# Trunk kernel: a third row pair of gate and up in seven products, T loaded first, and some pairs without accumulating DMA

## The chip, the cores and the metric

The kernel runs on one core of a Trainium2 chip. The core has a matrix engine (PE in the profile), a vector engine (DVE), a scalar engine (ACT), a general engine (POOL, GpSimd) and a sync engine (SP, which here only issues DMAs). Each of them works off its own list of instructions in order and waits on semaphores for the others. The metric is the device time of one execution in microseconds (us); lower is better.

## What is computed

The reference is a trunk of two residual layers on 256 tokens of width 2048, with float32 inputs and weights. Each layer is a token mixer (HGRN2 in layer 0, gated linear attention, GLA, in layer 1) together with a cross-attention into 256 memory tokens, an output projection, and a SwiGLU feed-forward part. Cut to what matters here:

```python
for layer in range(2):
    hn = _rmsnorm(h, norm_mix[layer])
    y, xq = _hgrn2_mixer(...) if layer == 0 else _gla_mixer(...)
    xa = _memory_attention(xq, mem_n, w_mem_kv[layer])
    h = h + concatenate([y, xa]) @ w_out[layer]
    hn = _rmsnorm(h, norm_ffn[layer])
    gate, up = split(hn @ w_gate_up[layer], 2)      # w_gate_up: 2048 x 11264
    h = h + (silu(gate) * up) @ w_down[layer]       # w_down: 5632 x 2048
return _rmsnorm(h, norm_final)
```

Nearly all of the work is products of the 256 tokens with weights that are read once from device memory.

## The kernel before

**Precision.** A float32 weight tile is split into a high and a low part (`split`, L276): ACT copies it rounded into the high part, and DVE (or, once a block, POOL, through `free_port`) subtracts to get the low part. A product of an activation factor (also in two parts) with a weight tile is then three matmuls of 128x128 by 128x512. Split tiles lie in a ring of six buffers (`parts`) or, if single, of two (`part`).

**Seven products instead of eight.** Two wanted results (for instance gate and up, or two column groups of one matrix) for two token tiles from two row tiles of weights form a 2x2 by 2x2 block product: eight products the plain way, seven by a Strassen-Winograd scheme. The kernel takes the 16 row tiles of a weight in eight *pairs* p = 0..7. A pair has one of three kinds:

- **O**: eight products. `raw` holds four weight tiles of 128x512, which are split in two halves a and b (two ACT casts and two DVE subtractions of 128x1024).
- **S**: seven products (`seven`, L427). DVE also forms sums of weight tiles: it needs T, the sum of the two c1 tiles, then T minus the c0 tile (a 128x512 subtraction on `raw`), two more differences (128x1024 on `raw`), and six split tiles instead of four (named a, b, c and d). T itself is made by DMA: after the plain loads, POOL issues a DMA that adds the second c1 tile onto `raw[:, 1]` (`accum_op=add`, L425).
- **H**: eight products that are spread over the same seven accumulators as S; DVE has one more subtraction and one more split tile than for O.

**The feed-forward part** (`ffn`, L1178) works in 11 blocks of 512 columns a layer. For each block `project_halves` (L597) runs through the eight pairs; a string of `KINDS` (L1167) gives their kinds: one string each for blocks 0 to 3, the last one for blocks 4 to 10. `PAIRS` (L360) says which sums of activation tiles are prepared for each pair: those of S (eight factors), of O (six, among them d1, which only O uses) or of both (B). H uses factors that S has too. After block b come two *downs* of earlier blocks (L1218): w_down times finished columns, accumulated onto h. Seven DVE additions (`sums`, L1187) put a block's seven accumulators together while the downs run. When a down is done, ACT copies its two results from the matrix engine's banks back to h (`give_back`, L1232).

**What sets the order.** From block 1 on (and from pair 3 of block 0) every engine's order is the program's own (`Engine.kept`); elsewhere a scheduler orders the instructions. Loads go through `load_pair` (L413), issued by SP, into a ring of three `raw` tiles of four weight tiles each: pair p+3 is loaded into the tile that pair p leaves when DVE has read it for the last time (its tile d for S). All compute instructions show as L151, a helper's line, so that groups are told apart by tile names: `f_p` are the accumulators of a block, `fd` those of a down, `partsNa` to `partsNd` the split tiles of load number N, `raw` the loaded tiles. In the GLA mixer `gg..p` and `gk..p` are accumulators.

`project_two` (L522) does the same for the mixers, the output projection and the last downs; there two or three pairs of a projection are S and the others plain.

Of the kernel before, what the change touches and what calls it, by code (L numbers as in the profile page):

```python
# [14 lines left out]
ALU = mybir.AluOpType  # L15
AX = mybir.AxisListType

P = 128
# [10 lines left out]
DK = 192  # L29
# [11 lines left out]
def trunk_kernel(ctx: ExitStack, tc: tile.TileContext, x, mem, norm_mix, norm_ffn, norm_mem,  # L41
                 norm_final, hgrn_w_in, hgrn_lb_logits, hgrn_onorm, gla_w_in, gla_w_gk,
                 gla_b_gk, gla_onorm, w_mem_kv, w_out, w_gate_up, w_down, c_ident, c_mask, out):
    nc = tc.nc
# [312 lines left out]

    PAIRS = "SSOSSOSB"  # L360
    HOMES = (("hq", "hq"),) * 4 + (("F", "K"), ("T", "sc"), ("Q", None), ("v", "gate"))
    FACTORS = {"S": ("x10", "x00", "x01", "x11", "s", "d0", "u", "z"), "O": ("x10", "x00", "x01", "x11", "d0", "d1"),
               "B": ("x10", "x00", "x01", "x11", "s", "d0", "u", "z", "d1")}
# [46 lines left out]

    TIMES = {"S": (1,) * 7, "O": (0, 2, 2, 2, 2, 0, 0), "H": (0, 2, 2, 2, 1, 0, 1)}

    def load_pair(raw, w, p, c0, c1, n, kind):  # L413

        if n_w[0] == 1:
            for k, j, c in ((0, 0, c0), (0, 1, c1), (1, 3, c0), (1, 2, c1)):
                nc.sync.dma_start(out=raw[:, j, 0:n], in_=w[(2 * p + k) * P:(2 * p + k + 1) * P, c:c + n])
                if k == 0 and c == c1:
                    load_mem(0, 256, 512)
            return  # L420
        for j, c in ((slice(1, 3), c1), (slice(0, 4, 3), c0)):
            nc.sync.dma_start(out=raw[:, j, 0:n],
                              in_=w[2 * p * P:(2 * p + 2) * P, c:c + n].rearrange("(k p) c -> p k c", p=P))
        if kind == "S":
            nc.gpsimd.dma_start(out=raw[:, 1, 0:n], in_=w[(2 * p + 1) * P:(2 * p + 2) * P, c1:c1 + n], accum_op=ALU.add)  # L425

    def seven(i, raw, between=None):  # L427

        n = raw.shape[2]
        tt = ve.tensor_tensor  # L430
        b00, = split(raw[:, 0:1, :], f"{i}a")
        b11, b10 = split(raw[:, 2:4, :], f"{i}b")
        if between:
            between()

        tt(out=raw[:, 0, :], in0=raw[:, 1, :], in1=raw[:, 0, :], op=ALU.subtract)
        tt(out=raw[:, 2:4, :], in0=raw[:, 2:4, :], in1=raw[:, 0:1, :].broadcast_to([P, 2, n]), op=ALU.subtract)
        t6, t7 = split(raw[:, 0:2, :], f"{i}c", turned=True)
        t5, t4 = split(raw[:, 2:4, :], f"{i}d")
        return {1: ("x00", b00), 2: ("x01", b10), 3: ("z", b11), 4: ("x11", t4), 5: ("s", t5), 6: ("u", t6), 7: ("d0", t7)}  # L440
# [79 lines left out]
            self.x = lambda k, t: quads[p // 2].x(p % 2 * 2 + k, t)  # L520

    def project_two(pairs, plan, w, c0, c1, n, name, give, view=lambda ps: ps, onto=None, prep=None, behind=None,  # L522
                    base=0):

        ps, out = {}, []  # L530
        if any(c.isdigit() for c in plan):
            order, plan = [base + int(c) for c in plan[::2]], plan[1::2]
        else:
            sevens, plains = iter(range(len(PAIRS))), iter(range(plan.count("S"), len(PAIRS)))
            order = [next(sevens if c == "S" else plains) for c in plan]
        left = {b: plan.count("S") * (b < 8) + 2 * plan.count("-") * (b in (2, 3, 4, 8)) for b in range(1, 9)}

        def product(b, left_factor, right):
            first = b not in ps
            if first:  # L540
                ps[b] = bank(f"{name}p{b}")
            left[b] -= 1
            (xh, xl), (hi, lo) = left_factor, right
            acc = ps[b][:, 0:n]
            pe.matmul(acc, xh, hi, start=first, stop=False)
            pe.matmul(acc, xh, lo, start=False, stop=False)
            pe.matmul(acc, xl, hi, start=False, stop=left[b] == 0)

        def add(to, b, other):
            ve.tensor_tensor(out=to, in0=view(ps[b][:, 0:n]), in1=other, op=ALU.add)  # L550

        def early():
            l, r = give()
            out.extend((l(0), l(1), r(0), r(1)))
            s0, s1, e1, e0 = out
            ac.copy(out=s0, in_=view(ps[1][:, 0:n]))
            add(e1, 6, s0)
            add(s1, 7, e1)
            add(e0, 5, s1)
            add(e1, 5, e1)  # L560
            if onto:
                for to, part in zip(onto, out):
                    ve.tensor_tensor(out=to, in0=to, in1=part, op=ALU.add)
                out[:] = onto

        for at, (p, kind) in enumerate(zip(order, plan)):
            i, raw = new_raw()
            if i == 0:
                load_pair(raw, w, p, c0, c1, n, kind)
            if prep:  # L570
                prep(at)
            if i > 0:
                load_pair(raw, w, p, c0, c1, n, kind)
            if kind == "S":
                todo = held(behind, seven, i, raw[:, :, 0:n]) if behind else seven(i, raw[:, :, 0:n])
                last = at == plan.rindex("S")
                for b in (1, 6, 7, 5, 2, 4, 3) if last else (3, 2, 1, 6, 7, 5, 4):
                    product(b, pairs[p].get(todo[b][0]), todo[b][1])
                if last and at == len(plan) - 1:
                    early()  # L580
                elif len(pending) > MANY:
                    step()
                continue
            b00, b01 = split(raw[:, 0:2, 0:n], f"{i}a", 2 if i else 1)
            b11, b10 = split(raw[:, 2:4, 0:n], f"{i}b")
            if at > 0 and at == plan.rindex("S") + 1:
                early()
            for k, (lf, rt) in enumerate(((b00, b01), (b10, b11))):
                step()
                for b, t, right_factor in ((2, 0, lf), (4, 1, lf), (8, 1, rt), (3, 0, rt)):  # L590
                    if b == 8 and len(pending) > MANY:
                        step()
                    product(b, pairs[p].x(k, t), right_factor)
        for to, b in zip(out, (2, 4, 3, 8)):
            add(to, b, to)

    def project_halves(forms, kinds, w, c0, c1, name, key, keep):  # L597


        left = {b: sum(TIMES[kind][b - 1] for kind in kinds) for b in range(1, 8)}  # L600
        ps = {}

        def product(b, left_factor, right):
            first = b not in ps
            if first:
                ps[b] = bank(f"{name}p{b}")
            left[b] -= 1
            (xh, xl), (hi, lo) = left_factor, right
            pe.matmul(ps[b], xh, hi, start=first, stop=False)
            pe.matmul(ps[b], xh, lo, start=False, stop=False)  # L610
            pe.matmul(ps[b], xl, hi, start=False, stop=left[b] == 0)

        for p, kind in enumerate(kinds):
            Engine.kept = keep <= p
            i, raw = new_raw()
            load_pair(raw, w, p, c0, c1, 512, kind)
            x = forms[p].get
            last = p == len(PAIRS) - 1
            if kind == "S":
                todo = seven(i, raw, lambda: mark(key + p))  # L620
                for b in (1, 2, 6, 7, 5, 4, 3) if last else (1, 3, 2, 6, 7, 5, 4):
                    product(b, x(todo[b][0]), todo[b][1])
            else:
                b00, b01 = split(raw[:, 0:2, :], f"{i}a")
                mark(key + p)
                b11, b10 = split(raw[:, 2:4, :], f"{i}b")
                todo = [[(2, "x00", b00), (5, "x10", b01), (4, "x10", b00), (3, "d0", b01)]]
                if kind == "O":
                    todo.append([(2, "x01", b10), (5, "x11", b11), (4, "x11", b10), (3, "d1", b11)])
                else:  # L630
                    ve.tensor_tensor(out=raw[:, 3, :], in0=raw[:, 3, :], in1=raw[:, 2, :], op=ALU.subtract)
                    e1, = split(raw[:, 3:4, :], f"{i}c")
                    todo.append([(2, "x01", b10), (3, "x01", b11), (7, "x11", b11), (4, "x11", e1)])
                todo = [m for ms in zip(*todo) for m in ms] if last else todo[0] + todo[1]
                for b, f, right in todo:
                    product(b, x(f), right)
            step()
        return ps
# [398 lines left out]
    def gla_pair(w, pr, dec, decay, hq, r, yq):  # L1037
# [40 lines left out]
        def give():  # L1078
            for name in "kq":
# [2 lines left out]
            return [lambda t, d=d: d[:, t, :, 0:DK] for d in dst]  # L1082

        project_two(hq["pairs"], ("------S-", "------S-")[pr], w, kw + pr * 2 * DK, pr * 2 * DK, 2 * DK, f"gk{pr}", give,
                    lambda ps: ps.rearrange("p (a c) -> p a c", c=DK))
        for d in dst:
            for t in range(NT):
                ac.activation(out=d[:, t, :, 0:DK], in_=d[:, t, :, 0:DK], func=AF.Copy, scale=r[:, t:t + 1])
# [7 lines left out]
        for a in range(2):  # L1096
            def give():
                for dst, tag in ((gate, "gate"), (v, "v")):
# [1 line left out]
                return [lambda t, d=d[a]: d[:, t, :] for d in (gate, v)]  # L1100

            project_two(hq["pairs"], GLA[pr][a], w, 2 * kw + MIX + (2 * pr + a) * DV, 2 * kw + (2 * pr + a) * DV, DV,
                        f"gg{pr}{a}", give)
            for dst, func in ((gate[a], AF.Silu), (v[a], AF.Copy)):
                for t in range(NT):
                    ac.activation(out=dst[:, t, :], in_=dst[:, t, :], func=func, scale=r[:, t:t + 1])
# [57 lines left out]
    PARTS = ((0,), (1, 2), (3, 4), (5, 6), (7, 8), (9, 10))  # L1164


    KINDS = ("SHOSHOSO", "HHOSSOSO", "SHOSSOSO", "SSOSSOHS", "SSOSSOSS")  # L1167

# [224 lines left out]
```

## Time and profile before

| what | us |
|---|---|
| median of three runs | 2276.28 |
| lowest and highest of them | 2270.11, 2280.8 |
| the profiled execution | 2272.82 |
| its span, from first to last instruction | 2271.0 |
| PE busy in the span | 2247.5 |
| DVE busy | 1974.3 |
| ACT busy | 1429.7 |
| POOL busy | 210.9 |

The profiled execution lies 3.46 us under the median of the runs and 1.82 us above its own span. The page gives each engine's busy time; the chain of waits follows the end of the program back to its start; the table of windows gives busy time by stretch; the timeline lists single instructions with the idle time before them and what ended it. The stages in time are: memory keys and values to about 105 us, the HGRN2 mixer to 422, output projection to 517, feed-forward of layer 0 to 1211, GLA mixer to 1484, output projection to 1574, feed-forward of layer 1 to the end. PE's granted clock is 1.00 or 0.99 in nearly all of these stretches.

### The profile page before, as it was taken

The page shows a single profiled execution, that of the slowest core. Times are in us where ns is not written, and L with a number is a line of the kernel's source. Part 1 is how long each engine was busy: PE and PEld are TensorE (multiplying, and loading weights), DVE is VectorE, ACT ScalarE, POOL GpSimd, SP SyncE. Part 2 cuts the span into 40 slices and gives each one's busy share as a digit, 9 for nine tenths or more (in the row PEclk, how much of TensorE's full clock was granted, in tenths as well). Part 3 has the DMA queues.
Part 4 walks back from the last instruction along what each step waited for, and adds up shares of the span by engine and source line. Part 5 has one row for each costly group of instructions (what it writes and reads, how often), then busy time and mean ns, then how long its engine had stood idle before and what let it go on. Part 6 is the DMA issues. An engine that isn't in the chain of part 4 may idle for free.

```text
span 2271.0 us, 30130 instructions
## 1 busy us (share of the span) xinstructions
PE 2247.5 (99%) x10710; PEld 1904.3 (84%) x10710; DVE 1974.3 (87%) x2449; ACT 1429.7 (63%) x1938; POOL 210.9 (9%) x215
## 2 busy tenths in 40 slices
PE   9999999999999999999999999999999999999998
PEld 7888888888888888888889899888888888888887
DVE  7889999898898889988996786789888898888997
ACT  7656656565666666666675565567566666666664
POOL 1000100000111111111100000000011111111110
PEclk9999999999999999999999999999999999999999
DMA  8656665656777777777765556466677777777774
GB/s 293 215 170 208 203 184 166 194 195 181 223 233 226 223 231 247 224 215 228 235 211 164 149 161 191 139 212 213 195 222 223 235 231 220 232 230 228 232 240 153
DMA packets 254827, 475.56 MB, mean 209 GB/s; under 512 B 15663, under 2 KB 46419, under 8 KB 254419
## 3 DMA queue, kind: packets, MB, share of 16 engines
q1 hardware_dynamic: 231203, 429.64, 56.1%
q0 software_dynamic: 22176, 39.72, 11.1%
q10 hardware_dynamic: 1296, 4.26, 0.5%
q8 instruction: 84, 1.38, 0.2%
q14 instruction: 68, 0.56, 0.1%
HBM read 470.42 MB, written 3.15 MB: 209 GB/s over the span
## 4 chain that ended last, share of the span: by engine, by line
PE 94%; DVE 2%; DMA 2%; issue 1%; ACT 0%; SPq 0%; POOL 0%; POOLq 0%; DVEq 0%; ACTq 0%
PE f_p L151 39%; PE fd L151 19%; PE wo L151 4%; PE m1p L151 2%; PE hv2p L151 2%; PE hv1p L151 2%; PE hv0p L151 2%; PE wo0p L151 2%; PE wo1p L151 2%; PE hf2p L151 2%; PE hf1p L151 2%; PE fd_0p L151 2%; PE m0p L151 2%; PE gg01p L151 1%; PE hf0p L151 1%; DMA raw<-in_gla_w_in_dram 1%
## 5 line engine op out<-in xcount | busy, mean ns | idle before, releaser
L151 DVE TENSOR_TENSOR raw<-raw 128x512 f32<-128x512 f32 (+3 forms) x320 | 299.0, 934 | 62.7 <-DMA raw<-in_w_gate_up_dram 34.0
L151 DVE TENSOR_TENSOR parts<-raw,parts 128x1024 fp32r<-128x1024 f32 (+1 forms) x196 | 224.3, 1179 | 23.4 <-ACT parts L151 23.0
L151 ACT CAST parts<-raw 128x1024 fp32r<-128x1024 f32 (+1 forms) x216 | 212.6, 1017 | 50.4 <-PE fd L151 6.5
L425 POOL DMA_DIRECT2D raw<-in_w_gate_up_dram x114 | 98.9, 867 | 990.2 <-DMA raw<-in_w_gate_up_dram 670.1
L151 ACT COPY h<-fd 128x512 f32<-128x512 f32 x80 | 46.6, 588 | 79.1 <-PE fd L151 75.8
L292 POOL TENSOR_TENSOR parts<-raw,parts 128x1024 fp32r<-128x1024 f32 x20 | 48.8, 2440 | 204.3 <-ACT parts L151 192.0
L151 ACT ACTIVATE s<-s,rf_r 128x512 f32<-128x512 f32 x44 | 31.8, 723 | 41.9 <-DVE s L151 41.7
L151 DVE TENSOR_TENSOR e<-f_p,e 128x512 f32<-128x512 f32 x66 | 45.3, 686 | 2.6 <-DVE s L151 0.5
L151 ACT COPY fd<-h 128x512 f32<-128x512 f32 x82 | 45.3, 585 | 0.0
L151 PE MATMUL fd<-parts,s_2h 128*128 128x512 f32 x128 | 39.8, 392 | 0.0
L151 PE MATMUL fd<-parts,s_0h 128*128 128x512 f32 x128 | 39.8, 392 | 0.0
L151 PE MATMUL fd<-parts,s_4h 128*128 128x512 f32 x128 | 39.8, 392 | 0.0
L151 PE MATMUL fd<-parts,s_8h 128*128 128x512 f32 x128 | 39.8, 392 | 0.0
L151 PE MATMUL fd<-parts,s_6h 128*128 128x512 f32 x128 | 39.8, 392 | 0.0
L151 PE MATMUL fd<-parts,s_3h 128*128 128x512 f32 x128 | 39.4, 389 | 0.0
L151 PE MATMUL fd<-parts,s_7h 128*128 128x512 f32 x128 | 39.4, 389 | 0.0
L151 PE MATMUL fd<-parts,s_5h 128*128 128x512 f32 x128 | 39.4, 389 | 0.0
L151 PE MATMUL fd<-parts,s_1h 128*128 128x512 f32 x128 | 39.4, 389 | 0.0
L151 DVE TENSOR_TENSOR s<-f_p,e 128x512 f32<-128x512 f32 x44 | 30.3, 690 | 10.1 <-PE f_p L151 8.2
L425 POOL DMA_DIRECT2D raw<-in_hgrn_w_in_dram x17 | 14.8, 872 | 216.0 <-DMA raw<-in_hgrn_w_in_dram 125.9
L151 DVE SCALAR_TENSOR_TENSOR s<-e,rf_r,s 128x512 f32<-128x512 f32 x44 | 31.0, 747 | 0.2
L151 PEld LDWEIGHTS fd<-parts,s_7h 128*128 128x128 f32 x128 | 24.0, 188 | 5.0
(5729 smaller groups left out, 7315.4 us busy)
## 6 DMA issues: line engine op xcount, KB each, us to landing
raw<-in_w_gate_up_dram SPq DMA_DIRECT2D x352, 512.0 KB, 4.2
raw<-in_w_down_dram SPq DMA_DIRECT2D x80, 1024.0 KB, 6.7
raw<-in_hgrn_w_in_dram SPq DMA_DIRECT2D x96, 512.0 KB, 4.2
raw<-in_gla_w_in_dram SPq DMA_DIRECT2D x96, 384.0 KB, 3.3
raw<-in_w_gate_up_dram POOLq DMA_DIRECT2D x114, 256.0 KB, 5.4
raw<-in_w_out_dram SPq DMA_DIRECT2D x16, 1024.0 KB, 5.2
raw<-in_w_out_dram SPq DMA_DIRECT2D x32, 512.0 KB, 4.1
raw<-in_w_mem_kv_dram SPq DMA_DIRECT2D x30, 512.0 KB, 5.6
```

Source lines behind the costliest of these rows:

```text
L151: ins = func(*args, **kwargs)
L292: low = (nc.gpsimd if free_port else ve).tensor_tensor(out=both[:, 1, k:j, 0:m], in0=src[:, k:j, :], in1=both[:, 0, k:j, 0:m].bitcast(F32) ...
L425: nc.gpsimd.dma_start(out=raw[:, 1, 0:n], in_=w[(2 * p + 1) * P:(2 * p + 2) * P, c1:c1 + n], accum_op=ALU.add)
```

## The change

There are three edits.

1. `PAIRS` and `KINDS`: pair 2 of gate and up is prepared as S instead of O. In blocks 4 to 10 it runs as S (seven products). In blocks 0 to 3 it becomes H (eight products, as O).
2. `load_pair` has a flag `fed`. An S pair that is fed now loads T's first tile by a DMA of its own ahead of all others, lets POOL add the second tile onto it, and loads c0's two tiles and the remaining c1 tile after that: three SP DMAs instead of two.
3. An S pair that is not fed has two plain DMAs and no accumulating one; DVE forms T with an addition in `seven`. Not fed are the first pair of each feed-forward block (`fed = p > 0`) and all S pairs of the GLA mixer's `project_two` calls.

```diff
-    PAIRS = "SSOSSOSB"
+    PAIRS = "SSSSSOSB"
...
-    def load_pair(raw, w, p, c0, c1, n, kind):
+    def load_pair(raw, w, p, c0, c1, n, kind, fed):
...
-        for j, c in ((slice(1, 3), c1), (slice(0, 4, 3), c0)):
-            nc.sync.dma_start(out=raw[:, j, 0:n],
-                              in_=w[2 * p * P:(2 * p + 2) * P, c:c + n].rearrange("(k p) c -> p k c", p=P))
-        if kind == "S":
-            nc.gpsimd.dma_start(out=raw[:, 1, 0:n], in_=w[(2 * p + 1) * P:(2 * p + 2) * P, c1:c1 + n], accum_op=ALU.add)
-
-    def seven(i, raw, between=None):
+        if kind == "S" and fed:
+            rows = [w[(2 * p + k) * P:(2 * p + k + 1) * P, c1:c1 + n] for k in range(2)]
+            nc.sync.dma_start(out=raw[:, 1, 0:n], in_=rows[0])
+            nc.gpsimd.dma_start(out=raw[:, 1, 0:n], in_=rows[1], accum_op=ALU.add)
+        nc.sync.dma_start(out=raw[:, 0:4:3, 0:n], in_=w[2 * p * P:(2 * p + 2) * P, c0:c0 + n].rearrange("(k p) c -> p k c", p=P))
+        if kind == "S" and fed:
+            nc.sync.dma_start(out=raw[:, 2, 0:n], in_=rows[1])
+        else:
+            nc.sync.dma_start(out=raw[:, 1:3, 0:n], in_=w[2 * p * P:(2 * p + 2) * P, c1:c1 + n].rearrange("(k p) c -> p k c", p=P))
+
+    def seven(i, raw, fed, between=None):
...
+        if not fed:
+            tt(out=raw[:, 1, :], in0=raw[:, 1, :], in1=raw[:, 2, :], op=ALU.add)
         tt(out=raw[:, 0, :], in0=raw[:, 1, :], in1=raw[:, 0, :], op=ALU.subtract)
...
     def project_two(pairs, plan, w, c0, c1, n, name, give, view=lambda ps: ps, onto=None, prep=None, behind=None,
-                    base=0):
+                    base=0, fed=True):
...
-            load_pair(raw, w, p, c0, c1, 512, kind)
+            fed = p > 0
+            load_pair(raw, w, p, c0, c1, 512, kind, fed)
...
         project_two(hq["pairs"], ("------S-", "------S-")[pr], w, kw + pr * 2 * DK, pr * 2 * DK, 2 * DK, f"gk{pr}", give,
-                    lambda ps: ps.rearrange("p (a c) -> p a c", c=DK))
+                    lambda ps: ps.rearrange("p (a c) -> p a c", c=DK), fed=False)
...
             project_two(hq["pairs"], GLA[pr][a], w, 2 * kw + MIX + (2 * pr + a) * DV, 2 * kw + (2 * pr + a) * DV, DV,
-                        f"gg{pr}{a}", give)
+                        f"gg{pr}{a}", give, fed=False)
...
-    KINDS = ("SHOSHOSO", "HHOSSOSO", "SHOSSOSO", "SSOSSOHS", "SSOSSOSS")
+    KINDS = ("SHHSHOSO", "HHHSSOSO", "SHHSSOSO", "SSHSSOHS", "SSSSSOSS")
```

On DVE, in one of the blocks 4 to 10 of layer 0, the rows from pair 1's last two split tiles (load 173) to pair 3's first (load 175) stood so before (`raw_N` is the loaded tile of a pair):

```order
L151 SCALAR_TENSOR_TENSOR parts173c<-raw_7945,parts173c 128x1024
L151 TENSOR_TENSOR parts173d<-raw_7945,parts173d 128x1024
L151 TENSOR_TENSOR parts174a<-raw_7990,parts174a 128x1024
L151 TENSOR_TENSOR parts174b<-raw_7990,parts174b 128x1024
L151 TENSOR_TENSOR parts175a<-raw_8023,parts175a 128x512
```

The same stretch of DVE's list in the changed kernel:

```order
L151 SCALAR_TENSOR_TENSOR parts173c<-raw_8046,parts173c 128x1024
L151 TENSOR_TENSOR parts173d<-raw_8046,parts173d 128x1024
L151 TENSOR_TENSOR parts174a<-raw_8092,parts174a 128x512
L151 TENSOR_TENSOR parts174b<-raw_8092,parts174b 128x1024
L151 TENSOR_TENSOR raw_8092<-raw_8092 128x512
L151 TENSOR_TENSOR raw_8092<-raw_8092 128x1024
L151 SCALAR_TENSOR_TENSOR parts174c<-raw_8092,parts174c 128x1024
L151 TENSOR_TENSOR parts174d<-raw_8092,parts174d 128x1024
L151 TENSOR_TENSOR parts175a<-raw_8132,parts175a 128x512
```

Pair 2 (load 174) has six DVE instructions where it had two, and the pairs 0 to 4 now form five S pairs in a row.

On SP, at the end of the same block, the loads of pairs 5, 6 and 7 and of the first down (two loads) stood so before (x2: two alike in a row):

```order
L422 DMA raw_8101<-in_w_gate_up_dram 128x2x512 x2
L422 DMA raw_8134<-in_w_gate_up_dram 128x2x512 x2
L422 DMA raw_8173<-in_w_gate_up_dram 128x2x512 x2
L303 DMA raw_8214<-in_w_down_dram 128x4x512
L303 DMA raw_8258<-in_w_down_dram 128x4x512
```

And in the changed kernel, from pair 6 to the first load of the down:

```order
L423 DMA raw_8245<-in_w_gate_up_dram 128x512
L425 DMA raw_8245<-in_w_gate_up_dram 128x2x512
L427 DMA raw_8245<-in_w_gate_up_dram 128x512
L423 DMA raw_8285<-in_w_gate_up_dram 128x512
L425 DMA raw_8285<-in_w_gate_up_dram 128x2x512
L427 DMA raw_8285<-in_w_gate_up_dram 128x512
L303 DMA raw_8327<-in_w_down_dram 128x4x512
```

Each fed pair has three loads; POOL's addition to `raw[:, 1]` waits for the first of them, the 128x512 one, as it waited for the first 128x2x512 one before.

On DVE, around the first S pair of the GLA mixer (load 230, 384 columns), the rows stood so before; `y_3l` is a part of the cross-attention's result and `raw` the loaded tile:

```order
L151 TENSOR_TENSOR parts229a<-raw_10347,parts229a 128x2x384
L151 TENSOR_TENSOR parts230a<-raw_10380,parts230a 128x384
L151 TENSOR_TENSOR raw_10380<-raw_10380 128x384
L151 TENSOR_TENSOR y_3l<-ao_10264,y_3h 128x512
L151 TENSOR_TENSOR y_3l<-ao_10271,y_3h 128x512
```

And in the changed kernel:

```order
L151 TENSOR_TENSOR parts230a<-raw_10519,parts230a 128x384
L151 TENSOR_TENSOR raw_10519<-raw_10519 128x384
L151 TENSOR_TENSOR parts229a<-raw_10486,parts229a 128x2x384
L151 TENSOR_TENSOR raw_10519<-raw_10519 128x384
L151 TENSOR_TENSOR y_3l<-ao_10403,y_3h 128x512
```

DVE has one row on `raw` more, the addition that forms T, and the split tile of the load before (229) has moved in between it and the subtraction that uses T.

More of the change, by code (lines that the diff above doesn't have):

```diff
@@ L568, in project_two @@
             if i == 0:
-                load_pair(raw, w, p, c0, c1, n, kind)
+                load_pair(raw, w, p, c0, c1, n, kind, fed)
             if prep:
@@ L572, in project_two @@
             if i > 0:
-                load_pair(raw, w, p, c0, c1, n, kind)
+                load_pair(raw, w, p, c0, c1, n, kind, fed)
             if kind == "S":
-                todo = held(behind, seven, i, raw[:, :, 0:n]) if behind else seven(i, raw[:, :, 0:n])
+                todo = held(behind, seven, i, raw[:, :, 0:n], fed) if behind else seven(i, raw[:, :, 0:n], fed)
                 last = at == plan.rindex("S")
@@ L619, in project_halves @@
             if kind == "S":
-                todo = seven(i, raw, lambda: mark(key + p))
+                todo = seven(i, raw, fed, lambda: mark(key + p))
                 for b in (1, 2, 6, 7, 5, 4, 3) if last else (1, 3, 2, 6, 7, 5, 4):
```

## The prediction

> **What bounds the kernel now.** I read the busy times first, then the windows, then the chain of waits.
>
> ```profile
> PE 2247.5 (99%) x10710; PEld 1904.3 (84%) x10710; DVE 1974.3 (87%) x2449; ACT 1429.7 (63%) x1938; POOL 210.9 (9%) x215
> 516.85:601.80 84.95, 84.95 (x383) 70.29 (x383) 74.76 (x89) 52.06 (x66) 8.36 (x8) 1.00 0.72 219
> 954.63:1016.73 62.10, 62.10 (x280) 51.53 (x279) 54.12 (x57) 39.40 (x49) 6.78 (x8) 1.00 0.72 217
> 1234.20:1484.00 249.80, 238.76 (x1402) 231.74 (x1401) 191.77 (x317) 146.14 (x229) 14.84 (x22) 0.99 0.55 163
> 971.83 5.46 PE fd L151 x24
> 977.29 39.44 PE f_p L151 x174
> 1016.73 16.32 PE fd L151 x72
> ```
>
> A window's columns are its length, then busy time of PE, PEld, DVE, ACT and POOL, PE's clock, DMA share and rate. PE is busy for all of 84.95 us of the first two blocks and all of 62.10 us of a late block, and the chain of a late block is PE alone: 174 matmuls of the block in 39.44 us, 0.2267 us each, then downs. Only the GLA mixer has idle PE time, 249.80 - 238.76 = 11.0 us. So the change can gain by fewer matmuls, and by up to 11.0 us in GLA; it can lose wherever DVE comes late for PE. DVE is busy for 54 of 62 us there and is the engine to be checked.
>
> **Fewer matmuls.** In 7 blocks of each of 2 layers one product, three matmuls, goes: 42 x 0.2267 = **9.5 us less**. A late block takes 39.44 - 0.68 = 38.76 us of PE, a product 0.68, an S pair 4.76 and an O pair 5.44. In blocks 0 to 3 H has as many products as O, and PE gains nothing.
>
> **DVE in a late block.** The timelines of ACT and DVE in the block above:
>
> ```profile
> 976.70 1.27 ACT L151 COPY h<-fd 128x512 f32<-128x512 f32 x2 [2.31 <-PE fd L151]
> 978.96 1.23 DVE L151 SCALAR_TENSOR_TENSOR parts173c<-raw,parts173c 128x1024 fp32r<-128x1024 f32 x1 [0.96 <-ACT parts173c L151]
> 981.23 1.22 DVE L151 TENSOR_TENSOR parts174a<-raw,parts174a 128x1024 fp32r<-128x1024 f32 x1
> 983.50 0.69 DVE L151 TENSOR_TENSOR parts175a<-raw,parts175a 128x512 fp32r<-128x512 f32 x1
> 989.53 0.69 DVE L151 TENSOR_TENSOR parts176a<-raw,parts176a 128x512 fp32r<-128x512 f32 x1
> 994.71 1.22 DVE L151 TENSOR_TENSOR parts176d<-raw,parts176d 128x1024 fp32r<-128x1024 f32 x1
> ...
> 1008.59 1.95 DVE L151 TENSOR_TENSOR raw<-raw 128x512 f32<-128x512 f32 x2 [2.35 <-DMA raw<-in_w_gate_up_dram]
> 1010.55 1.23 DVE L151 SCALAR_TENSOR_TENSOR parts179c<-raw,parts179c 128x1024 fp32r<-128x1024 f32 x1
> 1011.74 1.23 DVE L151 TENSOR_TENSOR parts179d<-raw,parts179d 128x1024 fp32r<-128x1024 f32 x1
> ```
>
> DVE can't run far ahead: ACT's copy of the last down waits for PE, and behind it ACT makes what DVE's tile 173c needs. So in every block DVE starts pair 2 (load 174) 981.23 - 977.29 = 3.94 us after PE has started pair 0. From there an O pair costs it 983.50 - 981.23 = 2.27 us and an S pair 989.53 - 983.50 = 6.03. Pair 2 as S costs 3.76 more. Pairs 2 to 7 are then S S S O S S: 5 x 6.03 + 2.27 = 32.42, and DVE could go on to the next work 36.36 us after PE's start. Its instructions overlap by some 0.09 us, so its last tile d is written at 36.45, and c 1.19 (1011.74 - 1010.55) before, at 35.26. PE starts pair 7 at 38.76 - 4.76 = 34.00 and uses c after two products, at 35.36, and d after four, at 36.72. **The margin is 0.1 us for c and 0.27 for d.** Before, d was ready at 1012.97 - 977.29 = 35.68, with the wait of 2.35 in it, and needed at 34.68 + 2.72 = 37.40: 1.7 us of margin. So the expected 9.5 us are all there if DVE waits for nothing in a block, and each tenth it waits beyond the first is a tenth of PE's, 14 times.
>
> **What DVE still waits for: T.** By the waits and the DMA issues:
>
> ```profile
> DVE raw L151 <- DMA raw<-in_w_gate_up_dram: 34.0, 42, 2.3
> raw<-in_w_gate_up_dram SPq DMA_DIRECT2D x352, 512.0 KB, 4.2
> raw<-in_w_gate_up_dram POOLq DMA_DIRECT2D x114, 256.0 KB, 5.4
> ```
>
> 42 waits of 0.81 us on average, at most 2.3, all in the subtraction that needs T. Pair 7 is the tightest: its tile is free when 176d ends at 995.93, and T is needed an O pair, an S pair and its own a and b (0.69 and 1.22, overlapping) later, 2.27 + 6.03 + 1.7 = 10.0 us; 4.2 + 5.4 at the medians, and some hand-over, fill that. With T's tile loaded alone and first, POOL's addition starts earlier by what 256 KB less take: 1.2 us at the 217 GB/s of the window above if the pair's loads flow one after the other, nothing if they share the engines and end together. I take the middle, 0.6. That leaves 0.2 of the average wait, and I put **0.25 us a block** on PE for it, 14 x 0.25 = 3.5 us back; the ends are 0 and 2.35 - 0.1 = 2.25.
>
> The Trainium skill (GPSIMD Engine Reference, Key points) says that GpSimd shares its SBUF interfaces with VectorE and contends with DVE instructions that have two SBUF inputs. Nearly all of DVE's here have two, and it will be denser; if that held POOL's descriptor writing back, T would come later and the sum would be that of the third rival below. The row that bears on it:
>
> ```profile
> L425 POOL DMA_DIRECT2D raw<-in_w_gate_up_dram x114 | 98.9, 867 | 990.2 <-DMA raw<-in_w_gate_up_dram 670.1 <-DVE raw L151 101.9 <-DVE h L151 32.6
> ```
>
> A mean of 867 ns beside a DVE that is busy 87% of the time shows no such stretching, so the sum goes without it.
>
> **First pairs and H.** DVE's addition for pair 0 (0.69 us, as the single `raw` subtraction below) comes before the point where DVE waits for ACT (0.96 at 978.96), which hides it; without that cover, and with DVE the bound everywhere, it would cost 0.69 us in each of 20 blocks, 13.8 us. H in place of O costs DVE there:
>
> ```profile
> 616.73 0.69 DVE L151 TENSOR_TENSOR raw<-raw 128x512 f32<-128x512 f32 x1
> 618.11 0.69 DVE L151 TENSOR_TENSOR parts103c<-raw,parts103c 128x512 fp32r<-128x512 f32 x1 [0.69 <-ACT parts103c L151]
> 650.39 0.69 DVE L151 TENSOR_TENSOR s<-f_p,e 128x512 f32<-128x512 f32 x1 [1.79 <-PE f_p L151]
> ```
>
> That is 0.69 + 0.69 of waiting + 0.69 = 2.07 us in 8 blocks. In such a block DVE itself waits 1.79 us for PE before the sums, so I cost it at nothing; the 0.3 that stick out would be 2.2 us in all, the whole without cover 16.6. Pair 2's larger activation form is two small instructions more, twice, beside a PE that is never idle there: nothing. The loads' new order in HGRN2, memory and output projection changes no DVE work, and PE has no wait there that it could remove: nothing, with -1 to +2 for the scheduler's order.
>
> **GLA.** Ten accumulating DMAs go, ten DVE additions of 128x384 come:
>
> ```profile
> L151 DVE TENSOR_TENSOR raw<-raw 128x384 f32<-128x384 f32 x10 | 5.6, 557 | 14.2 <-DMA raw<-in_gla_w_in_dram 10.1 <-issue 3.2 <-DVE parts237a L151 0.5
> PE slg L151 <- DVE GQ L151: 3.5, 2, 2.3
> PE slg L151 <- ACT GQ L151: 2.4, 1, 2.4
> PE tgk L151 <- ACT gsk L151: 1.8, 2, 1.0
> PE zp L151 <- DVE gk L151: 1.8, 1, 1.8
> PE ty L151 <- DVE ggate L151: 1.0, 1, 1.0
> PE ty L151 <- DVE gro_v L151: 0.5, 1, 0.5
> ```
>
> And from the chain of waits there:
>
> ```profile
> 1254.81 5.57 DMA raw<-in_gla_w_in_dram
> ...
> 1263.47 1.99 PE zp L151 x8
> ...
> 1413.56 4.50 DMA raw<-in_gla_w_in_dram
> ...
> 1426.47 1.13 PE slg L151 x8
> ...
> 1456.47 2.84 DMA raw<-in_gla_w_in_dram
> ...
> 1465.15 0.76 PE ty L151 x5
> ```
>
> DVE loses waits of 14.2 us for T and gets 5.6 us of additions. PE's 11.0 idle us are its six rows (3.5 + 2.4 + 1.8 + 1.8 + 1.0 + 0.5 = 11.0), waits for what DVE and ACT make. In the chain zp (1.8), an slg (2.4, and 1.2 of the 3.5) and ty (1.0 and 0.5) stand some 10 us behind an addition's landing: 6.9 us; tgk and the other slg follow other work. Some of it comes back as DVE's additions. I take **6 us less**, between 11.0 less and 5.6 more (all additions on the path).
>
> **Sum.** -9.5 + 3.5 - 6 = -12.0. Against the profiled execution, 2272.82, that is 2260.8; the median of the runs shown lies 3.5 higher, so the median after is forecast at **2264**.
>
> **Rivals.** (1) *Everything hides*: T in time in every block and all of PE's idle time in GLA gone: -9.5 - 11.0 = -20.5, 2256. For it: POOL is nearly idle. Against: the margin of 0.1 us. (2) *GLA gives nothing*: DVE's additions eat what the waits gave, since ACT's splits bound DVE there too: -6.0 to -0.4, about 2272. (3) *T is as late as before*: the first load is earlier, but the addition now runs beside the pair's other 768 KB, which were nearly all in before.
>
> ```profile
> q0 software_dynamic: 537, 0.97, 19.5%
> ```
>
> By the DMA view of 980 to 1012 us, 0.97 MB of additions took 19.5% of its 32 us: 6.2 us, 1.7 for 256 KB. If packets of both queues alternate, T takes up to 1.7 us longer; at half of that, 0.25 + 0.85 = 1.1 us a block, -9.5 + 15.4 - 6 = 0, 2276. The Trainium skill (DMA: Bandwidth & Descriptors, Queues, rings and completion order) says that each engine goes round robin between its queues packet by packet, which speaks for this rival. (4) *DVE bound*, the other side: pair 7's T comes 2.25 us late in all 14 blocks, as it did once at 1008.59, now with no margin: -9.5 + 31.5 - 6 = +16, 2292. It turns the change slower by over 0.5% from 1.9 us a block on ((11.4 + 15.5) / 14). Against it: most waits were near 0.8.
>
> **How the numbers follow.** Forecast 0.47, (1) 0.15, (2) 0.15, (3) 0.13, (4) 0.10. About 0.5% (11.4 us) is what a measurement of this kernel can tell from no change. The forecast case spreads over 2260 to 2269 and lies beyond 11.4 us in a little over half; with (1) that gives 0.41 faster, (4) gives 0.10 slower, the rest is 0.49. The range takes in (1), (2) and (3) with the spread of the runs and leaves out (4): 2255 to 2281.
>
> **What would show it.** PE's row of a late block at 38.8 us from its first matmul to the down says that DVE keeps up; 39.1 that 0.25 us is right; over 39.8 that T is late, and then the wait in pair 7's (or 6's) first subtraction on `raw` must be named DMA and be over a microsecond. If PE waits at tiles c or d with no DMA wait on DVE, the margin was miscounted. GLA's window should be some 6 us shorter, with zp's wait gone. POOL's 867 ns must not grow. Wrong it would be if DVE's step for an S pair in a row of five is not 6.03, or if ACT, 63% busy now, sets it.

## The result and the profile after

The changed kernel runs in 2269.56 us (median of 20 runs), the kernel before, beside it, in 2275.12 (20 runs): a ratio of 0.9976 with an interval of 0.997 to 0.9983. The change gains 5.6 us, where 12 were forecast. The profiled execution after takes 2269.23 us with a span of 2267.5, so the spans differ by 3.5 us. Busy times after:

```profile
PE 2242.7 (99%) x10668; PEld 1892.7 (83%) x10668; DVE 2049.6 (90%) x2555; ACT 1451.1 (64%) x1974; POOL 195.8 (9%) x199
```

The windows by stage say where the 3.5 us are. Columns: start and end, length, then busy time of PE, PEld, DVE, ACT and POOL, PE's clock, DMA share, rate. The rows are blocks 0 to 3, blocks 4 to 10 ("late"), the end of layer 0, GLA with its output projection, and the same two groups of blocks in layer 1. Before:

```profile
516.69:728.75 212.06, 212.06 (x956) 175.84 (x955) 186.55 (x208) 134.12 (x170) 21.81 (x20) 1.00 0.71 218
728.75:1163.40 434.65, 434.65 (x1947) 360.64 (x1946) 392.06 (x413) 283.30 (x346) 53.27 (x49) 1.00 0.75 230
1163.40:1208.26 44.86, 44.86 (x211) 37.40 (x210) 38.22 (x60) 28.01 (x48) 1.20 (x2) 1.00 0.52 167
1208.26:1574.30 366.04, 355.00 (x2024) 331.59 (x2023) 287.87 (x451) 220.88 (x343) 20.11 (x29) 1.00 0.57 174
1574.30:1786.37 212.07, 212.07 (x956) 175.79 (x955) 186.97 (x209) 134.42 (x170) 21.86 (x20) 1.00 0.71 220
1786.37:2221.02 434.65, 434.65 (x1947) 360.52 (x1946) 392.25 (x414) 283.79 (x346) 53.27 (x49) 1.00 0.76 229
```

And after:

```profile
516.68:730.60 213.92, 213.13 (x957) 175.45 (x955) 193.41 (x219) 136.35 (x174) 19.24 (x17) 1.00 0.69 211
730.60:1169.11 438.51, 433.33 (x1926) 356.02 (x1925) 417.90 (x444) 291.31 (x358) 53.27 (x49) 1.00 0.77 228
1169.11:1215.52 46.41, 45.27 (x212) 37.35 (x210) 40.61 (x63) 28.62 (x49) 1.21 (x2) 1.00 0.52 166
1215.52:1569.10 353.58, 352.05 (x2025) 330.19 (x2023) 292.78 (x464) 220.79 (x343) 11.01 (x19) 1.00 0.55 175
1569.10:1781.71 212.61, 212.50 (x956) 175.61 (x955) 193.21 (x219) 136.26 (x174) 19.64 (x18) 1.00 0.69 214
1781.71:2217.52 435.81, 432.34 (x1927) 356.03 (x1926) 418.39 (x445) 291.45 (x358) 53.26 (x49) 1.00 0.77 229
```

GLA's row is 12.46 us shorter. The late blocks have 21 matmuls fewer in each layer (1947 to 1926) and are yet longer, by 3.86 and 1.16 us. Blocks 0 to 3 lose 1.86 and 0.54, the end of layer 0 loses 1.55. Together +3.86 + 1.16 + 1.86 + 0.54 + 1.55 - 12.46 = -3.5.

A late window without any stall would be 434.65 - 21 x 0.2267 = 429.89 us. So PE stalls (438.51 - 429.89) + (435.81 - 429.89) = 14.5 us in 14 blocks, **1.04 us a block**. PE's timeline at the end of one block, the one that the prediction walked through (load 179 is its pair 7), shows the place:

```profile
1016.34 0.39 PE L151 MATMUL f_p<-parts179b,hf_7l 128*128 128x512 f32 x1
1017.36 0.49 PE L151 MATMUL f_p<-parts179c,hf_7h 128*128 128x512 f32 x1 [0.63 <-ACT parts179c L151]
1018.62 0.50 PE L151 MATMUL f_p<-parts179c,hf_7h 128*128 128x512 f32 x1 [0.76 <-DVE parts179c L151]
1018.96 0.40 PE L151 MATMUL f_p<-parts179c,hf_7l 128*128 128x512 f32 x1
```

Matmuls follow each other by 0.23 us; the three starts 1016.34, 1017.36 and 1018.62 are over a microsecond apart. PE waits for tile c of pair 7: first for its high part (ACT), then for its low part (DVE). The chain of waits behind that tile (start, length, what):

```profile
1007.35 7.95 DMA raw<-in_w_gate_up_dram
...
1015.38 0.70 DVE raw L151
...
1016.11 1.23 DVE raw L151
...
1017.34 1.23 DVE parts179c L151
...
1018.62 3.51 PE f_p L151 x14
```

It goes back to POOL's addition for T: issued at 1007.35, 7.95 us to its landing. DVE was at that place earlier and waited 1.92 us for it. In the table of waits (us in total, times, longest) DVE's line is shorter than before, but what is left now costs PE time:

```profile
DVE raw L151 <- DMA raw<-in_w_gate_up_dram: 17.6, 15, 3.4
```

And on the page, POOL's group of additions (busy, mean ns, idle before them) and their DMA issues (KB, median us to landing):

```profile
L424 POOL DMA_DIRECT2D raw<-in_w_gate_up_dram x108 | 93.7, 867 | 921.4 <-DMA raw<-in_w_gate_up_dram 366.6
raw<-in_w_gate_up_dram POOLq DMA_DIRECT2D x108, 256.0 KB, 4.3
```

34.0 us in 42 waits are 17.6 in 15: 13 of the 15 are pair 7 of a late block, the longest (3.4) pair 7 of block 3. The addition's median from issue to landing is better (4.3, was 5.4); its issue takes 867 ns as before. POOL's timeline has two issues at the end of this block, those of pairs 6 and 7:

```profile
1000.69 0.86 POOL L424 DMA_DIRECT2D raw<-in_w_gate_up_dram  x1 [10.46 <-DVE raw L151]
1007.35 0.86 POOL L424 DMA_DIRECT2D raw<-in_w_gate_up_dram  x1 [5.79 <-issue]
```

The view of line 424 in that stretch gives the time of the two to their landing (least, median, most):

```profile
DMA to landing us min/median/max: 4.2/6.1/7.9
```

Pair 6's addition (1000.69) took 4.2 us, with the other 768 KB of its own pair issued ahead of it; pair 7's (1007.35) took 7.9, with the same. What is different is on SP's queue:

```profile
1003.46 0.34 SPq L423 DMA_DIRECT2D raw<-in_w_gate_up_dram  x1
...
1005.73 6.40 SPq L303 DMA_DIRECT2D raw<-in_w_down_dram  x2
```

2.3 us behind pair 7's first load, at 1005.73, SP issues 1 MB of w_down, the down's first load (x2: the second follows 6 us later): pair 5 is an O pair, DVE is through with it in 2.27 us, and its tile comes free at once. So the 1 MB is on its way when POOL issues its addition, 1.6 us later. In all 14 late blocks pair 7's additions take 6.3 to 8.0 us, those of pairs 3, 4 and 6 from 4.0 to 4.4.

The DMA view of 1007.35 to 1010.00 us, the 2.65 us from the issue of pair 7's addition on, has one queue of data only, SP's:

```profile
q1 hardware_dynamic: 467, 0.92, 100.4%
```

No packet of the addition moves in that time, and 0.92 MB of plain loads do. Over the 14 blocks the first packet of pair 6's addition comes 1.56 us after its issue and the last 2.3 us after that; for pair 7 the two are 2.9 and 3.7 us in the mean. So the addition both starts late and is drawn out.

### The profile page after: what moved, and what is told of

Read it like the earlier page. It is cut to its first block, busy times and chain, and to the rows that moved or that the text cites. A ratio compares the mean times of both kernels' runs of the same rounds, so it can differ in the third digit from the quotient of the medians.

```text
span 2267.5 us, 30263 instructions
## 1 busy us (share of the span) xinstructions
PE 2242.7 (99%) x10668; PEld 1892.7 (83%) x10668; DVE 2049.6 (90%) x2555; ACT 1451.1 (64%) x1974; POOL 195.8 (9%) x199
## 3 DMA queue, kind: packets, MB, share of 16 engines
q0 software_dynamic: 19872, 36.18, 10.7%
## 4 chain that ended last, share of the span: by engine, by line
PE 66%; DVE 17%; issue 7%; DMA 7%; ACT 3%; SPq 0%; DVEq 0%; POOLq 0%; ACTq 0%; POOL 0%
PE fd L151 16%; PE f_p L151 14%; DVE raw L151 5%; DMA raw<-in_w_gate_up_dram 5%; PE wo L151 4%; PE m1p L151 2%; PE hv2p L151 2%; PE hv1p L151 2%; PE hv0p L151 2%; PE hf0p L151 2%; PE wo0p L151 2%; PE wo1p L151 2%; PE hf2p L151 2%; PE hf1p L151 2%; PE gk0p L151 1%
## 5 line engine op out<-in xcount | busy, mean ns | idle before, releaser
L151 DVE TENSOR_TENSOR raw<-raw 128x512 f32<-128x512 f32 (+2 forms) x386 | 349.7, 906 | 31.4 <-DMA raw<-in_w_gate_up_dram 17.6
L424 POOL DMA_DIRECT2D raw<-in_w_gate_up_dram x108 | 93.7, 867 | 921.4 <-DMA raw<-in_w_gate_up_dram 366.6
```

The lines of the kernel that those rows point to most:

```text
L151: ins = func(*args, **kwargs)
L424: nc.gpsimd.dma_start(out=raw[:, 1, 0:n], in_=rows[1], accum_op=ALU.add)
```

## The experiments

Two theories of the 1.04 us. A: the down's 1 MB slows pair 7's addition. B, the third rival on record: the pair's own 768 KB do. Beside them stands a third: DVE is too slow by its own work. "The stall" is worked out from the two late windows as above, and spread over the 14 blocks. All ratios are against the kernel before, run on the same chip.

### The O pair moved from pair 5 to pair 6

```diff
-    PAIRS = "SSSSSOSB"
+    PAIRS = "SSSSSSOB"
-    KINDS = ("SHHSHOSO", "HHHSSOSO", "SHHSSOSO", "SSHSSOHS", "SSSSSOSS")
+    KINDS = ("SHHSHSOO", "HHHSSSOO", "SHHSSSOO", "SSHSSHOS", "SSSSSSOS")
```

> The changed kernel, with pair 6 as the O pair in place of pair 5 (all strings of kinds have their positions 5 and 6 exchanged): the same products, the same DVE work, but the tile that the down's first load of 1 MB waits for comes free 3.8 us later, behind an S pair. Theory A (pair 7's T is late because this 1 MB flows beside POOL's addition, which takes 6.3 to 8.0 us there against 4.1 to 4.4 for pairs 3, 4 and 6): the addition of pair 7 takes some 4.3 us, DVE's wait for T is gone in the late blocks, PE's stall falls from 1.04 to about 0.1 us a block, and the time is some 13 us below the changed kernel, 2256 to 2258 us. Theory B (the third rival on record: the addition is slowed by the pair's own 768 KB): the addition still takes about 7 us and the time stays near 2269. Against both: the down's load, 3.8 us later, may make PE wait at the down.

Measured: 2279.13 us, ratio 1.0016 (1.0007 to 1.0025). The view of the additions' line over the same block's two last ones, of pairs 5 and 7:

```profile
DMA to landing us min/median/max: 4.1/4.1/4.1
```

The down's first load is issued after pair 7's addition (1012.22) now, as SP's timeline shows (x3: the first of three):

```profile
1015.02 8.66 SPq L303 DMA_DIRECT2D raw<-in_w_down_dram  x3
```

Pair 7's addition takes 4.1 us, and 4.1 to 4.5 in all late blocks; DVE waits for none of them. A was right on the transfer, B was not. But the time went up. PE's timeline at pair 5 (load 177):

```profile
1012.61 0.50 PE L151 MATMUL f_p<-parts177c,hf_5h 128*128 128x512 f32 x1
1013.87 0.50 PE L151 MATMUL f_p<-parts177c,hf_5h 128*128 128x512 f32 x1 [0.76 <-DVE parts177c L151]
```

1.26 us between two starts instead of 0.23. With six S pairs in a row, at 6.03 us a pair on DVE and 4.76 on PE, PE catches up with DVE in pair 5 already, before the O pair (2.27 on DVE, 5.44 on PE) gives DVE its time back. A stall of 1.2 us in every late block came from DVE's own work in place of the wait for T, and blocks 0 to 3 took 5.1 us more in layer 0 and 4.4 in layer 1 than in the changed kernel. The expectation had left DVE's place of catching up out.

### Pair 7's early product moved ahead

```diff
-                for b in (1, 2, 6, 7, 5, 4, 3) if last else (1, 3, 2, 6, 7, 5, 4):
+                for b in (1, 2, 3, 6, 7, 5, 4) if last else (1, 3, 2, 6, 7, 5, 4):
```

> The changed kernel, with pair 7's third product (tile b, ready early) moved from the last place to the third, ahead of those that need tile c. If PE's 1.04 us a block are a wait for tile c alone, 0.68 us of it is covered wherever it is longer: 14 blocks give 8.3 us, about 2261 us, with POOL's addition as slow as before (some 7 us). If PE waits for d as well, or DVE is behind by its own work, little is gained: 2266 to 2270.

Measured: 2266.32 us, ratio 0.9959 (0.9946 to 0.9971), 3 us under the changed kernel, not 8 (the late windows of the two profiled executions differ by 1.4). In this profile T landed 0.25 us later in the mean, and the end of the block has a new wait. ACT's timeline in the same block:

```profile
1015.63 1.06 ACT L151 ACTIVATE parts179c<-raw 128x1024 fp32r<-128x1024 f32 x1 [3.49 <-DVE raw L151]
...
1019.68 0.58 ACT L151 COPY e<-f_p 128x512 f32<-128x512 f32 x1
1020.16 1.11 ACT L151 COPY fd<-h 128x512 f32<-128x512 f32 x2
```

And PE's timeline where its block ends and the down begins:

```profile
1020.42 0.39 PE L151 MATMUL f_p<-parts179d,hf_7l 128*128 128x512 f32 x1
1020.80 0.73 PE L151 MATMUL fd<-parts,s_5h 128*128 128x512 f32 x2
```

The down starts by ACT's copy of h into its bank, and ACT, which waited 3.49 us for T too, gets to it only at 1020.16; PE's first matmul of the down starts at 1020.80, about when the first of the two copies is through, 0.38 after the matmul before it. In the mean of the 14 blocks DVE waits 1.18 us for T and PE stalls 0.69 in the block, so that the product covers 0.6; but PE loses 0.24 at the start of the down. So the product gains some 0.3 us a block of a late T, not 0.68: ACT comes late by the same wait.

### The mixer alone

The kernel before, with `fed=False` in the two GLA calls and nothing else.

> The kernel before, with only the GLA mixer's S pairs not fed (plain loads and DVE's addition); loads, first pairs and kinds are as before. The changed kernel's trace says that PE lost 11 us less there: about 2264 us. The prediction's term says 6 less: 2269. If the gain in the changed kernel came with the new load order, less than either.

Measured: 2263.07 us, ratio 0.9947 (0.9935 to 0.9959): 12 us less than before, more than either number. The window of GLA with the output projection:

```profile
1208.96:1564.64 355.68, 352.37 (x2025) 330.19 (x2024) 292.85 (x461) 221.12 (x343) 11.39 (x19) 1.00 0.55 174
```

All waits of PE in GLA there (us in total, times, longest):

```profile
PE spg L151 <- DVE GQ L151: 1.6, 1, 1.6
PE tgk L151 <- ACT gsk L151: 1.4, 2, 0.8
PE pxg L151 <- DVE GQ L151: 0.3, 1, 0.3
```

Of 11.0 us of waits 3.3 are left (1.4 in the changed kernel, both in tgk). **This edit is the whole gain of the change; the rest of the change costs 6 us** (2269.56 against 2263.07; the profiled spans differ by 6.6).

### The third pair alone

The kernel before with the changed `PAIRS` and `KINDS`.

> The kernel before, with only the new strings of pairs and kinds (pair 2 in seven products); loads and feeding as before. The prediction holds that T's own first load brings T 0.6 us earlier: without it PE would stall 1.04 + 0.6 us in each of 14 late blocks, 23 us against 9.5 us fewer products and some 2 in the first blocks: about 2291. If that load brings nothing, the stall is 1.04 as in the changed kernel and the time is 2280 to 2283. If T comes earlier in the old order, under 2276.

Measured: 2323.7 us, ratio 1.0212 (1.0191 to 1.0234), worse than any expectation. The late windows:

```profile
734.23:1184.87 450.64, 439.05 (x1927) 356.32 (x1926) 414.02 (x437) 291.08 (x356) 58.44 (x55) 1.00 0.77 225
1812.42:2265.91 453.49, 438.76 (x1926) 354.92 (x1925) 413.35 (x436) 290.06 (x355) 58.46 (x55) 1.00 0.76 225
```

DVE's timeline where a late block begins, at pair 0's subtraction that needs T:

```profile
984.71 1.95 DVE L151 TENSOR_TENSOR raw<-raw 128x512 f32<-128x512 f32 x2 [2.71 <-DMA raw<-in_w_gate_up_dram]
```

The stall is (450.64 + 453.49 - 2 x 429.89) / 14 = 3.2 us a block. DVE loses time to T at both ends of a block, 2.71 us at pair 0 and 1.3 at pair 7 of this one, and with five S pairs in a row it can't make up for either: PE stalls by 1.8 us in pairs 3 and 4 of this block and by 1.5 in pair 7. The next two runs take the two remedies away one at a time.

### Old order of loads; first pair fed

The first run is the changed kernel with the two loads and the addition of before in `load_pair`, the second has `fed = True` in `project_halves`.

> The changed kernel with the loads of every pair in their old order (1 MB in two loads, c1 first; POOL's addition behind the first of them); kinds, first pairs and the GLA mixer as changed. By the prediction T's own first load is worth 0.6 us in each late block: +8 us, 2278. By the run with only the third pair, in which POOL issued pair 7's addition only some 30.3 us into the block and T landed 35.2 us into it (33.2 in the changed kernel, DVE can use it at 32.3), the old order costs some 2 us in each of 14 late blocks, and less in the first ones: 2295 to 2302.

> The changed kernel with the first pair of each feed-forward block fed by POOL's addition again (T's tile loaded first); all else as changed. If T of the first pair is in time with the new order of loads, DVE loses its addition of 0.69 us a block, hidden in part: 2266 to 2270. If it is late as in the run with only the third pair (a wait of 2.71 us at a block's start), DVE starts each block some 2 us later and, with no margin at the end, PE stalls by that: 14 x 2 us, 2290 to 2300.

Measured: old loads 2279.8 us, ratio 1.002 (1.0011 to 1.0029); first pair fed 2271.17, ratio 0.9985 (0.9975 to 0.9994). Late windows of the run with old loads:

```profile
731.60:1169.97 438.37, 433.26 (x1926) 356.02 (x1925) 416.74 (x441) 290.78 (x356) 53.33 (x49) 1.00 0.76 227
1785.85:2224.32 438.47, 433.50 (x1926) 356.04 (x1925) 416.65 (x441) 290.90 (x356) 53.33 (x49) 1.00 0.76 228
```

With old loads the stall is (438.37 + 438.47 - 859.78) / 14 = 1.22 us, against 1.04. Over the 14 blocks POOL issues pair 7's addition 28.6 us after the block's start instead of 26.2, and it takes 4.75 us instead of 6.96: T lands at 33.3 instead of 33.15. **T's own first load starts the addition 2.4 us earlier and gains 0.2 us**, since the earlier addition is issued 1.6 us behind the down's 1 MB in place of 4.0. Of the 10 us between the medians the profiled spans show 6.8 (2274.3 against 2267.5): 2.5 in the late blocks and some 4 elsewhere, which weren't followed further.

Feeding the first pair costs some 2 us if T is loaded first: DVE then waits for that T in 5 of the 14 late blocks, by 0.3 to 1.9 us, where with the third pair alone it waits in all 14, by 0.9 to 3.3. So each of the two remedies alone does most of the work. Their separate costs (10 and 2 us) are far below the some 42 that they cost together (2323.7 less 2269.6 and less the mixer's 12).

### Pair 7 not fed, alone and with the early product

```diff
-            fed = p > 0
+            fed = 0 < p < 7
```

> The changed kernel with pair 7 not fed either: two plain loads and DVE's addition. DVE's tile c then comes 0.6 us later by its own work, and waits for no accumulating DMA. PE's stall should be 0.7 us in every late block in place of 1.04 on average (0.13 to 2.03): 5 us less, 2265. If the plain loads of pair 7 are late as well beside the down's 1 MB, DVE still waits for a DMA there and nothing is gained.

> Both edits: pair 7 not fed, and its third product ahead of those of tile c. The early product covered some 0.55 us of a wait in its own run, where T's lateness grew by 0.25 us by chance; here T's lateness is gone and 0.7 - 0.55 = 0.15 us of stall is left in a late block: 14 x (1.04 - 0.15) = 12.5 us under the changed kernel, 2257. If the loads are late, 2262 to 2266.

Measured: 2263.43 us, ratio 0.995 (0.9938 to 0.9963), and with both edits **2258.47 us, ratio 0.9929 (0.9916 to 0.9941)**. Late windows of the first, then of the second run:

```profile
730.82:1165.63 434.81, 432.14 (x1927) 356.10 (x1925) 422.13 (x451) 291.68 (x358) 47.24 (x42) 1.00 0.75 225
1778.63:2213.49 434.86, 432.15 (x1926) 356.10 (x1925) 422.22 (x451) 291.50 (x358) 47.22 (x42) 1.00 0.75 225
```

```profile
730.23:1163.09 432.86, 432.58 (x1926) 355.83 (x1925) 422.04 (x451) 291.66 (x358) 47.28 (x42) 1.00 0.75 225
1774.64:2207.25 432.61, 432.51 (x1927) 355.75 (x1925) 422.08 (x451) 291.79 (x358) 47.25 (x42) 1.00 0.75 226
```

Stalls of 0.71 and 0.41 us a block. In the first run PE's seven stalls in pair 7 of layer 0 are 0.65 to 0.70 and one of 0.94: the scatter from 0.13 to 2.03 in the 14 late blocks of the changed kernel went with the addition. DVE waits for no load of gate and up in these blocks; plain loads are in time beside the down's 1 MB. Of the 0.41 in the second run, 0.09 lie in the block and the rest at the start of the down, where PE waits for ACT's copy of h; there were to be 0.15 in all.

So with pair 7 not fed the third pair only breaks even with the mixer's edit alone (2263.43 against 2263.07), and the early product makes it a gain. The second version beats both kernels: 17 us under the one before, 11 under the changed one.

## Why the prediction was wrong

**Fewer matmuls, -9.5: right.** 42 matmuls fewer, and no late block has other work on PE.

**DVE's pace and margins: right to 0.2 us.** DVE's timeline of the changed kernel:

```profile
991.31 0.68 DVE L151 TENSOR_TENSOR parts175a<-raw,parts175a 128x512 fp32r<-128x512 f32 x1
997.33 0.68 DVE L151 TENSOR_TENSOR parts176a<-raw,parts176a 128x512 fp32r<-128x512 f32 x1
```

S pairs in a row step by 6.02 us, and ACT doesn't set it. Margin of tile c: forecast 0.1 us; measured, the stall is the wait for T plus 0.1, a margin of -0.1. The difference is in the zero of the count. The prediction took 977.29 from the chain as PE's start of pair 0; that is where the down's last matmul ends, and PE's timeline before has the block's first matmul starting under it:

```profile
977.12 0.61 PE L151 MATMUL f_p<-parts172a,hf_0h 128*128 128x512 f32 x2
```

Counted from 977.12, DVE's tile is written 0.17 later, at 35.43, and PE uses it at 35.36. With T formed by DVE, 0.6 later, the stall was 0.65 to 0.70 in most blocks.

**The wait for T, +3.5: here it failed**, with +14.5 measured, 13.3 of it DVE's waits for pair 7's T (0.95 a block) and the rest the margin above. The step is "T's tile loaded alone and first ... POOL's addition starts earlier by what 256 KB less take", 0.6 us, "that leaves 0.2 of the average wait". Two things in it were wrong. The average of 0.81 was over all 42 waits, where pair 7's own in the late blocks of before were 0.97 in the mean; and the earlier start was taken as an earlier end. After the change the mean wait of pair 7 is 0.95 us: T did not come earlier at all against DVE. The addition did start earlier, by 2.4 us, and took 2.2 longer (the run with the old loads). The old order hid in its lateness that the down's load was partly through when the addition began: before, pair 7's addition was issued 2.4 to 4.8 us behind the down's load and took 4.5 to 6.5, the longest where it followed closest; in the changed kernel 1.3 to 2.2 behind it, and 6.3 to 8.0.

**Third rival: right in the result, wrong in the cause.** It held 1.1 us a block, T as late as before, at 13%; 1.04 was measured. But it blamed the pair's own 768 KB, and additions behind these alone take 4.2 us; the moved O pair showed that it is the load of the next stage, which the prediction did not have among its queues though SP's list in the text on the change shows it right behind pair 7's loads. The Trainium skill (DMA: Bandwidth & Descriptors, Queues, rings and completion order) says that a DMA engine goes round between its queues packet by packet. The 7.9 us beside the down's load agree with it in so far as both queues move data from 1010.0 on; that the addition's first packet comes 2.65 us after its issue in place of 1.56 is not explained here. The pair's own loads, issued 3 to 4 us ahead of the addition, show no such cost, so the rule has to be asked for each transfer by its time of issue. The other rule, that GpSimd contends with VectorE for SBUF (the Trainium skill, GPSIMD Engine Reference, Key points), shows no effect on POOL's issue: 867 ns with DVE at 87% and at 90%.

**First pairs: right, for more than it said.** The first pair's addition on DVE costs nothing that shows (2269.56 with, 2271.17 without). That feeding it in the old order costs so much with the new kinds (most of some 42 us) was not foreseen.

**H and blocks 0 to 3, 0 with an end at 2.2: +2.4 measured**, of it some 0.8 in block 3 of layer 0, whose pair 7 waits 3.4 us for T, the rest in blocks 0 and 1, where the runs don't take H apart from the rest. The end of layer 0 lost 1.55, forecast as nothing in -1 to +2 for all such places: PE waits 1.1 us for DVE's h there, and waited for nothing before; why h is late stays open.

**GLA, -6: mis-sized.** The edit alone gives 12 us by the runs' medians, 10.4 by the windows. The step took only the waits that in the chain stand behind an addition's landing (6.9 us) and took off some for DVE's work. In fact nearly all of the 11.0 went, tgk's 0.4 and both slg waits with it: in the windows 9.5 us less of idle PE. The other 3 us of the 12.46 are PE's busy time, 355.00 before and 352.05 after for the same matmuls. Over half of that is the clock. In the profiled execution before, PE's granted clock was at 0.50 for 3.41 us in this mixer, right behind two waits of 1.03 and 0.80 us in tgk (the window's clock is the third number from the end):

```profile
1284.97:1288.38 3.41, 3.41 (x15) 3.31 (x14) 1.96 (x4) 2.75 (x6) 0.00 (x0) 0.50 0.74 235
```

Half of 3.41 is 1.7 us. The changed kernel and the mixer's edit alone have no such stretch in the mixer. Of 36 executions of the kernel before beside the experiments 33 list a mean clock of 0.996 to 0.998, while the profiled one has 0.999 and all five of the mixer's edit 0.999; so more such stretches may be behind the larger gain by the medians, which one trace can't show. One caution: in the run with the third pair alone, whose mixer is that of before, the same six waits come to 7.4 us, not 11.0, so part of these waits belongs to the execution profiled.

So the forecast of -12.0 became -3.5 by 11 us more of waiting for T, 4 us in places costed at nothing, and 6.5 us more gained in GLA, which hid nearly half of the other errors; that part was luck. The medians differ by 5.6, since the profiled execution before is faster than most of its kernel's. The fourth rival (slower) needed 1.9 us a block and did not come; with the third pair alone the stall was 3.2.

## What to carry to other kernels

A transfer that is issued earlier need not land earlier; here 2.4 us were worth 0.2, because a bigger load was then nearer ahead of it. Before counting the gain, list what all queues send in the microseconds up to the landing, the next stage's loads too. When an engine works through a block with a margin near zero, take the wait at its last step, not the mean over all steps, and rather spend 0.6 us of its own sure work than wait for a transfer whose time scatters by 1.7. An edit with several parts is worth taking apart even where the sum is a gain: here one part gave 12 us and the others took 6 back until pair 7 was mended.

## What the runs showed of the hardware

An accumulating DMA takes the DMA engines longer than a plain one of the same size. Queues of the changed kernel (packets, MB, share of 16 engines' time):

```profile
q1 hardware_dynamic: 233411, 429.65, 56.7%
q0 software_dynamic: 19872, 36.18, 10.7%
```

A packet of q0, whose 36.18 MB are 138 additions of 256 KB, holds 1.82 KB and takes 0.107 x 16 x 2267.5 us / 19872 = 195 ns of an engine; a packet of q1, 1.84 KB, takes 88 ns. Whether that is the addition's price or the software queue's can't be told, as no other transfers use q0. Behind the 768 KB of its own pair an addition of 256 KB lands after 4.0 to 4.4 us (pairs 3, 4 and 6 of the late blocks), with 1 MB more issued 1.3 to 2.2 us ahead of it after 6.3 to 8.0. Why it scatters by 1.7 us from block to block while the down's load is issued 24.55 or 24.56 us after each block's start stays open.

PE's granted clock can halve behind short waits. With the third pair alone it was at 0.50 for 3.41 us three times; one of them, from 1095.55 us on, came behind waits of 1.25 and 0.76 us at tile c of a pair 7, and matmuls then followed each other by 0.43 us instead of 0.23. Waits of 0.63 and 0.76 us at the same place of the changed kernel brought none. What decides it is not shown.
